# One weight block of 512 columns for the first 256 features of the feed-forward layers

## The chip, the core and the metric

The kernel runs on one core of a Trainium2 chip. The metric is the device time of one launch in microseconds (us), lower is better. The engines named below are TensorE (PE, matmuls), ScalarE (ACT), VectorE (DVE), GpSimd (POOL) and SyncE (SP, which issues the loads of the weights). An engine works through its own instructions in a fixed order, and waits at an instruction until the semaphores that it names have come.

## What is computed

Two layers on 256 tokens of 1024 features, all in float32. Each layer is a feed-forward half-step, a token mixer and a second feed-forward half-step; the mixer is gated linear attention in the first layer and a gated delta rule in the second.

```python
def swiglu(h, w_in, w_out):                       # w_in 1024 x 5632, w_out 2816 x 1024
    g, u = jnp.split(h @ w_in, 2, axis=-1)
    return (jax.nn.silu(g) * u) @ w_out

for i in range(2):
    x = x + 0.5 * swiglu(rmsnorm(x, norm_w[i, 0]), ffn_w_in[i, 0], ffn_w_out[i, 0])
    h = rmsnorm(x, norm_w[i, 1])
    x = x + (gla_mixer if i == 0 else gdn_mixer)(h, ...)
    x = x + 0.5 * swiglu(rmsnorm(x, norm_w[i, 2]), ffn_w_in[i, 1], ffn_w_out[i, 1])
return rmsnorm(x, final_norm_w)
```

The change touches the product `h @ w_in` for the first 256 of the 2816 features: 256 gate columns of g and 256 value columns of u.

## The kernel before

Six stages follow each other: f00, gla, f01, f10, gdn, f11 (a feed-forward layer is f and its layer and half). Every float32 product is made of three matmuls in a faster format: a weight is split into a rounded high part `hi` and the rest `lo`, the normalized and transposed activations `xT` likewise, and the products are xT high by hi, xT high by lo and xT low by hi.

The class `Weights` (`W`) feeds all stages with one stream of weight parts, numbered through the program (the four of the first columns of f01 are parts 99 to 102, for instance). SP loads raw blocks of 1 MB or 512 KB into 4 rotating buffers (`RAWS`). A part is 128 x 1024 values of a block: ACT rounds it to `hi` (line 69), DVE subtracts to get `lo` (line 76). 7 parts are kept (`LOOK`). The program text asks for the casts at chosen places: `high(n, held)` makes up to n casts on ACT, but none beyond `taken - held + LOOK`, where `taken` is the number of parts that `W.take` has handed out so far; `low` makes the next one on DVE. If `take` finds its part not yet cast, it makes it on the spot. So how many parts have been taken when `high` is called decides how far the casts run ahead, and with that in which place among an engine's other work each later cast stands.

Within a stage the 256 tokens are two halves, t = 0 and t = 1. A stage opens with its first columns, both halves over the same four weight parts; the opening is written out by hand in `step_over` (end of the stage before, transposes, `fill` of the first units of t = 0, then `low()` and `high(2, 4)`) and `second_half` (the rest of t = 0, `st.first(0)`, the units of t = 1 with `mids` between them, `st.first(1)`). `first` takes the accumulated columns out of PSUM: in a feed-forward layer with a Silu on ACT and a multiplication on DVE (lines 461 and 463), in gla with a scaled copy on ACT (line 623), in gdn with a Silu on ACT. The first stage has its own opening near the end of `trunk`.

In gla and gdn the first columns are `first_columns`: four parts of 2 row blocks (k) by 512 columns, matmuls of 512 columns, one PSUM buffer of two banks (`gup`) per half of the tokens of which one bank is used. In a feed-forward layer they are `FeedForward.part`: four parts of 4 row blocks by 256 columns (gate and value parts by turns, c = 0 and 1), matmuls of 256 columns (lines 445 to 447), one `gup` buffer per half with gate columns in one bank and value columns in the other. After the first columns, a feed-forward layer goes on with `ps_f` (lines 341 and 342: a matmul of 512 and one of 256 columns by turns, one part for each buffer); its matmul order is made by a scheduler of the framework from the program's dependencies. gla goes on with its gates, `ps_gk` and `tm_v` columns; gdn with convolved columns `ps_d` (lines 576 to 578, hi, hi, lo), for which DVE does a convolution (line 947) and copies (line 936), and with a chain on POOL and DVE that inverts triangular matrices (`Lm`, lines 1012 to 1034).

Of the kernel before, what the change touches and what calls it, by code (L numbers as in the profile page):

```python
# [11 lines left out]
AF = mybir.ActivationFunctionType  # L12
# [3 lines left out]
P = 128  # L16
# [11 lines left out]
class Weights:  # L28
# [15 lines left out]
    def _load(self, upto):  # L44
        while self.loaded < min(upto + 1, len(self.raws)):
            src, shape = self.raws[self.loaded]
            t = self.raw_pool.tile([P, 2048], F32, tag="raw", name=f"raw{self.loaded}")
            n = shape[0] * shape[1]
            tv = t[:, :n].rearrange("p (a b) -> p a b", b=shape[1])
            self.nc.sync.dma_start(tv, src)  # L50
            self.raw_tiles[self.loaded] = tv
            self.loaded += 1
# [55 lines left out]
def trunk(ctx: ExitStack, tc: tile.TileContext, x_in, norm_w, ffn_w_in, ffn_w_out, gla_w_in, gla_w_gk, gla_b_gk,  # L108
# [59 lines left out]
    for st in stages:  # L168
        if st[0] == "f":
            w1, w2 = ffn_w_in[int(st[1]), int(st[2])], ffn_w_out[int(st[1]), int(st[2])]  # L170
            for i in range(2):
                for c in (0, FF):
                    sub_rows(blk(w1, i * 512, 512, c, 256), 0, 4, 256)
            wo = {}
# [207 lines left out]
    def first_columns(N, name, pss):  # L382

        parts = []

        def units(t):
            if t == 0:
                parts.extend(W.take() for _ in range(4))
            pss[t] = gup(f"tm_{name}{t}")[:, 0, :]
            for s in range(4):  # L390
                for k in range(2):
                    xh, xl = (N.xT[:, 2 * s + k, u + t * P:u + (t + 1) * P] for u in (0, 256))
                    hi, lo = parts[s]
                    nc.tensor.matmul(pss[t], lhsT=xh, rhs=hi[:, k, :], start=(s + k == 0), stop=False)
                    nc.tensor.matmul(pss[t], lhsT=xh, rhs=lo[:, k, :], start=False, stop=False)
                    nc.tensor.matmul(pss[t], lhsT=xl, rhs=hi[:, k, :], start=False, stop=(s == 3 and k == 1))
                    yield
                if t == 1:
                    low()
                    high(1, 3 - s)  # L400

        return units

# [24 lines left out]
    class FeedForward:  # L428
        factor, quarter, mids = 0.5, 4, {}

        def __init__(self, N):
            self.N, self.parts, self.ps, self.am, self.aTs = N, [], {}, [], {}

        def part(self, t, s, c):

            N, i = self.N, 2 * s + c
            while len(self.parts) <= i:
                self.parts.append(W.take())
            if t not in self.ps:
                self.ps[t] = gup(f"g0_{N.name}{t}")  # L440
            hi, lo = self.parts[i]
            for k in range(4):
                o = self.ps[t][:, c, 0:256]
                xh, xl = (N.xT[:, 4 * s + k, u + t * P:u + (t + 1) * P] for u in (0, 256))
                nc.tensor.matmul(o, lhsT=xh, rhs=hi[:, k, :], start=(s + k == 0), stop=False)  # L445
                nc.tensor.matmul(o, lhsT=xh, rhs=lo[:, k, :], start=False, stop=False)  # L446
                nc.tensor.matmul(o, lhsT=xl, rhs=hi[:, k, :], start=False, stop=(s == 1 and k == 3))  # L447
                yield

        def units(self, t):  # L450
            for s in range(2):
                for c in range(2):
                    yield from self.part(t, s, c)
                    if t == 1:
                        low()
                        high(1, 3 - 2 * s - c)

        def first(self, t):
            N, ps = self.N, self.ps[t]
            sl = small(f"sl0_{N.name}{t}", 256, tag="t1")  # L460
            nc.scalar.activation(sl, ps[:, 0, 0:256], AF.Silu, scale=N.r[t][:, 0:1])
            a = small(f"a0_{N.name}{t}", 256, tag="t1")
            nc.vector.scalar_tensor_tensor(a, ps[:, 1, 0:256], N.r[t][:, 0:1], sl, op0=ALU.mult, op1=ALU.mult)
            self.am.append(a)
            if t == 1:
                rows_bc(N)
# [128 lines left out]
    def gla(N):  # L595
# [29 lines left out]
        ps0 = {}  # L625
        st.units = first_columns(N, "v0", ps0)
        st.first = lambda t: v_evac(ps0[t], t, 0)
# [204 lines left out]
    def gdn(N):  # L832
# [62 lines left out]
        ps0, ev0 = {}, gate_evac(N, srn, 0, 4, nwb[:, 256:384])  # L895
        st.units = first_columns(N, "dr0", ps0)
        st.first = lambda t: hold.update({"finish": ev0(ps0[t], t, t == 1)})
# [563 lines left out]
    with manual():  # L1461
# [7 lines left out]
        if isinstance(st, FeedForward):  # L1469
            part = lambda *a: [None for _ in st.part(*a)]  # L1470
            part(0, 0, 0)
            for g in range(2):
                turn_x(N, 1, g)()
                high(1)
                low()
            part(0, 0, 1)
            parameters()
            rms(N, 0)
            for c in range(2):
                part(1, 0, c)  # L1480
            rms(N, 1)
            high(1)
            low()
            for t in range(2):
                for c in range(2):
                    part(t, 1, c)
                st.first(t)
                high(1)
                low()
# [50 lines left out]
```

## Time and profile before

| | |
|---|---|
| median of 3 runs | 1045.27 us (1044.95 to 1045.68) |
| the profiled execution | 1045.1 us, its span 1043.4 us, granted clock 0.998 |
| busy in the span | PE 1027.3, PE weight loads 892.0, DVE 701.0, ACT 590.4, POOL 212.6 us |
| weights and data moved | 180.26 MB, mean 173 GB/s |
| stages | f00 to about 195 us, gla to 308, f01 to 495, f10 to 682, gdn to 848, f11 to the end |

Times in the rows are us from the start of the span. A row of the timeline gives the start, the duration, the engine, the line and the operation, what is written and read, and, in brackets, how long the engine had been idle before and what ended that. Matmuls overlap: the time that one takes in a row of matmuls is the step from its start to the next one's start, which is shorter than its duration. "x2" means that the row stands for two instructions, one behind the other.

### The profile page before, as it was taken

Reading aid. Unit: us, or ns where it says so; the run is one execution under the profiler, and the core shown is the slowest. Engines: PE = TensorE matmul, PEld = TensorE weight load, DVE = VectorE, ACT = ScalarE, POOL = GpSimd, SP = SyncE. Lnnn points to the kernel's source line nnn. Section 1 sums busy time; section 2 is a strip of 40 time slices with the busy share of each in tenths; the row PEclk is TensorE's granted clock in tenths of the full one; section 3 lists DMA queues with packets and bytes.
Section 4 is the critical chain, followed back from the end, with each engine's and each line's share of the span. In section 5 each row is a group of like instructions: output and inputs, shape, how many; then the busy total and the mean of one; then the engine's idle time right before and its main releaser. Section 6 shows DMA issues by size and latency. Waiting matters only on the chain.

```text
span 1043.4 us, 15585 instructions
## 1 busy us (share of the span) xinstructions
PE 1027.3 (98%) x6162; PEld 892.0 (85%) x6162; DVE 701.0 (67%) x956; ACT 590.4 (57%) x1019; POOL 212.6 (20%) x250
## 2 busy tenths in 40 slices
PE   8999999999999999999999999999999999999996
PEld 8888888789889888888988888879989898888885
DVE  5866666666577666666766666578998776666664
ACT  7655555573556555555655555478677565555552
POOL 2111111103201111110111111117734401111111
PEclk9999999999999999999999999999999999999999
DMA  8764645444364564744564655544443156556431
GB/s 295 242 235 139 231 158 172 155 130 158 141 222 162 202 212 152 240 139 148 210 233 155 209 175 188 164 125 135 144 135 131 47 198 240 191 173 216 147 122 41
DMA packets 132410, 180.26 MB, mean 173 GB/s; under 512 B 5212, under 2 KB 111760, under 8 KB 132336
## 3 DMA queue, kind: packets, MB, share of 16 engines
q1 hardware_dynamic: 131712, 178.14, 51.0%
q0 software_dynamic: 416, 0.84, 0.4%
q8 instruction: 48, 0.79, 0.3%
q10 hardware_dynamic: 208, 0.29, 0.1%
q14 instruction: 26, 0.21, 0.1%
HBM read 178.20 MB, written 1.05 MB: 172 GB/s over the span
## 4 chain that ended last, share of the span: by engine, by line
PE 91%; DVE 3%; POOL 2%; issue 1%; DMA 1%; ACT 1%; SPq 0%; POOLq 0%; DVEq 0%; ACTq 0%
PE ps_f L341 29%; PE ps_f L342 15%; PE acc_f L414 7%; PE acc_f L413 7%; PE acc_f L415 7%; PE ps_d L576 2%; PE g_f L445 1%; PE g_f L447 1%; PE g_f L446 1%; PE ps_d L578 1%; PE ps_d L577 1%; DMA x<-in_x_dram 1%; POOL Mc L1002 1%; DVE lo L76 1%; PE acc_gdn L415 1%
## 5 line engine op out<-in xcount | busy, mean ns | idle before, releaser
L76 DVE TENSOR_TENSOR lo<-raw,hi 128x1024 fp32r<-128x1024 f32 x336 | 431.4, 1297 | 198.8 <-ACT hi L69 198.7
L69 ACT CAST hi<-raw 128x1024 fp32r<-128x1024 f32 x338 | 348.1, 1046 | 190.6 <-PE acc_f L415 83.7
L341 PE MATMUL ps_f<-xT_f,hi 128*128 128x512 f32 x1280 | 455.6, 398 | 0.0
L342 PE MATMUL ps_f<-xT_f,lo 128*128 128x256 f32 x1280 | 359.1, 281 | 0.0
L341 PEld LDWEIGHTS ps_f<-xT_f,hi 128*128 128x128 f32 x1280 | 240.5, 188 | 58.4
L342 PEld LDWEIGHTS ps_f<-xT_f,lo 128*128 128x128 f32 x1280 | 241.7, 189 | 2.8
L371 POOL TENSOR_TENSOR pair_f<-plo_f,Rb_f 128x512 f32<-128x512 f32 x76 | 102.8, 1352 | 558.6 <-DVE plo_f L369 558.6
L413 PE MATMUL acc_f<-hi,aT_f 128*128 128x512 f32 x352 | 138.4, 393 | 0.0
L414 PE MATMUL acc_f<-lo,aT_f 128*128 128x512 f32 x352 | 137.9, 392 | 0.0
L415 PE MATMUL acc_f<-hi,aT_f 128*128 128x512 f32 x352 | 137.0, 389 | 0.0
L413 PEld LDWEIGHTS acc_f<-hi,aT_f 128*128 128x128 f32 x352 | 66.1, 188 | 15.1
L415 PEld LDWEIGHTS acc_f<-hi,aT_f 128*128 128x128 f32 x352 | 66.1, 188 | 14.4
L414 PEld LDWEIGHTS acc_f<-lo,aT_f 128*128 128x128 f32 x352 | 66.1, 188 | 10.7
L405 ACT CAST aT_f<-a_f 128x256 fp32r<-128x256 f32 x80 | 32.5, 407 | 71.6 <-DVE a_f L483 71.4
L481 ACT ACTIVATE sl_f<-pair_f 128x256 f32<-128x256 f32 x80 | 33.5, 418 | 54.6 <-POOL pair_f L371 48.6
L369 DVE TENSOR_TENSOR plo_f<-ps_f,plo_f 128x512 f32<-128x512 f32 x80 | 54.7, 683 | 12.6 <-ACT plo_f L368 12.5
L406 DVE TENSOR_TENSOR aT_f<-a_f,aT_f 128x256 fp32r<-128x256 f32 x80 | 34.0, 425 | 36.0 <-ACT aT_f L405 36.0
L576 PE MATMUL ps_d<-xT_gdn,hi 128*128 128x256 f32 x192 | 56.5, 294 | 0.1
L578 PE MATMUL ps_d<-xT_gdn,lo 128*128 128x256 f32 x192 | 54.4, 283 | 1.1 <-DVE lo L76 1.1
L577 PE MATMUL ps_d<-xT_gdn,hi 128*128 128x256 f32 x192 | 54.2, 282 | 0.0
L368 ACT COPY plo_f<-ps_f 128x512 f32<-128x512 f32 x80 | 46.4, 580 | 12.8 <-PE ps_f L342 12.8
L483 DVE TENSOR_TENSOR a_f<-sl_f,pair_f 128x256 f32<-128x256 f32 x80 | 33.0, 413 | 10.4 <-ACT sl_f L481 10.4
(363 smaller groups left out, 1299.0 us busy)
## 6 DMA issues: line engine op xcount, KB each, us to landing
raw<-in_ffn_w_in_dram SPq DMA_DIRECT2D x80, 1024.0 KB, 5.4
raw<-in_ffn_w_out_dram SPq DMA_DIRECT2D x44, 1024.0 KB, 5.4
raw<-in_gdn_w_in_dram SPq DMA_DIRECT2D x16, 1024.0 KB, 5.4
raw<-in_gla_w_in_dram SPq DMA_DIRECT2D x12, 1024.0 KB, 5.1
raw<-in_ffn_w_in_dram SPq DMA_DIRECT2D x16, 512.0 KB, 3.5
raw<-in_gla_w_out_dram SPq DMA_DIRECT2D x4, 1024.0 KB, 5.0
raw<-in_gdn_w_out_dram SPq DMA_DIRECT2D x4, 1024.0 KB, 5.0
out_dram<-fin SPq DMA_DIRECT2D x3, 256.0 KB, 2.1
```

The lines of the kernel that those rows point to most:

```text
L69: nc.scalar.copy(hv, src)
L76: self.nc.vector.tensor_tensor(lv, src, hv.bitcast(F32), op=ALU.subtract)
L341: nc.tensor.matmul(ps, lhsT=hi[:, k, :], rhs=N.xT[:, k, :], start=(k == 0), stop=False)
L342: nc.tensor.matmul(ps[:, 0:256], lhsT=lo[:, k, :], rhs=N.xT[:, k, 0:256], start=False, stop=(k == KT - 1))
L369: nc.vector.tensor_tensor(t, ps[:, :, 0:256], t, op=ALU.add)
L371: (eng or nc.gpsimd).tensor_tensor(dst, t, N.Rb.unsqueeze(1).broadcast_to([P, 2, 256]), op=ALU.mult)
L413: nc.tensor.matmul(accs[t][n], lhsT=ah, rhs=hi[:, 0, c], start=first, stop=False)
L414: nc.tensor.matmul(accs[t][n], lhsT=ah, rhs=lo[:, 0, c], start=False, stop=False)
L415: nc.tensor.matmul(accs[t][n], lhsT=al, rhs=hi[:, 0, c], start=False, stop=last)
L576: nc.tensor.matmul(o, lhsT=hi[:, k, :], rhs=xh, start=(k == 0), stop=False)
L577: nc.tensor.matmul(o, lhsT=hi[:, k, :], rhs=xl, start=False, stop=False)
L578: nc.tensor.matmul(o, lhsT=lo[:, k, :], rhs=xh, start=False, stop=(k == KT - 1))
```

## The change

The raw blocks of the first 256 features hold 2 row blocks by 256 gate and 256 value columns (two load instructions each) instead of 4 row blocks by 256 columns of one kind. A feed-forward layer now uses `first_columns`, with matmuls of 512 columns. `first_columns` asks for one `gup` buffer for both halves of the tokens, t = 0 in its first bank and t = 1 in its second, and takes a weight part from `W` when its first matmul is written instead of all four at the start; both hold for gla and gdn too. The lines of the new file stand 5 lower at its top and 11 higher further on (the cast `lo` is line 81, the first columns lines 401 to 403, `ps_f` lines 346 and 347).

```diff
@@ Weights._load
-            self.nc.sync.dma_start(tv, src)
+            if len(src.shape) == 3:
+                self.nc.sync.dma_start(tv, src)
+            else:
+
+                for a in range(shape[0]):
+                    self.nc.sync.dma_start(tv[:, a, :].rearrange("p (c f) -> p c f", c=src.shape[2]), src[:, a])
@@ the weight stream
-            for i in range(2):
-                for c in (0, FF):
-                    sub_rows(blk(w1, i * 512, 512, c, 256), 0, 4, 256)
+            for i in range(4):
+                w4 = w1[i * 256:(i + 1) * 256, :].rearrange("(k p) (c f) -> p k c f", p=P, c=2)
+                sub_rows(W.add_raw(w4[:, :, :, 0:256], (2, 512)), 0, 2, 512)
@@ first_columns
+        def part(t, s):
+            while len(parts) <= s:
+                parts.append(W.take())
+            if not pss:
+                both = gup(f"tm_{name}")
+                pss.update({0: both[:, 0, :], 1: both[:, 1, :]})
+            for k in range(2):
+                xh, xl = (N.xT[:, 2 * s + k, u + t * P:u + (t + 1) * P] for u in (0, 256))
+                hi, lo = parts[s]
+                nc.tensor.matmul(pss[t], lhsT=xh, rhs=hi[:, k, :], start=(s + k == 0), stop=False)
+                nc.tensor.matmul(pss[t], lhsT=xh, rhs=lo[:, k, :], start=False, stop=False)
+                nc.tensor.matmul(pss[t], lhsT=xl, rhs=hi[:, k, :], start=False, stop=(s == 3 and k == 1))
+                yield
+
         def units(t):
-            if t == 0:
-                parts.extend(W.take() for _ in range(4))
-            pss[t] = gup(f"tm_{name}{t}")[:, 0, :]
             for s in range(4):
-                for k in range(2):
...
-                    yield
+                yield from part(t, s)
                 if t == 1:
                     low()
                     high(1, 3 - s)
 
-        return units
+        return part, units
@@ FeedForward
-        factor, quarter, mids = 0.5, 4, {}
+        factor, quarter, mids = 0.5, 2, {}
...
+            self.part, self.units = first_columns(N, f"g0_{N.name}", self.pss)
@@ FeedForward.first
-            nc.scalar.activation(sl, ps[:, 0, 0:256], AF.Silu, scale=N.r[t][:, 0:1])
+            nc.scalar.activation(sl, ps[:, 0:256], AF.Silu, scale=N.r[t][:, 0:1])
-            nc.vector.scalar_tensor_tensor(a, ps[:, 1, 0:256], N.r[t][:, 0:1], sl, op0=ALU.mult, op1=ALU.mult)
+            nc.vector.scalar_tensor_tensor(a, ps[:, 256:512], N.r[t][:, 0:1], sl, op0=ALU.mult, op1=ALU.mult)
```

PE in f01, where the first columns pass from t = 0 to t = 1 (`g0_f010` and `g0_f011` are their buffers; `hi99` to `hi102` are the four parts, 103 is the next one). Before:

```order
1609 L447 MATMUL g0_f010_2861<-hi102_2793,xT_f01_2796 128x256
1610 L445 MATMUL g0_f010_2861<-hi102_2793,xT_f01_2796 128x256
1611 L446 MATMUL g0_f010_2861<-lo102_2794,xT_f01_2796 128x256
1612 L447 MATMUL g0_f010_2861<-hi102_2793,xT_f01_2796 128x256
1613 L445 MATMUL g0_f011_2955<-hi99_2733,xT_f01_2796 128x256 [waits Activation_49]
1614 L446 MATMUL g0_f011_2955<-lo99_2734,xT_f01_2796 128x256
1615 L447 MATMUL g0_f011_2955<-hi99_2733,xT_f01_2796 128x256 [waits DVE_49]
```

The same place on PE after the change (one buffer `tm_g0_f01` for both halves):

```order
1539 L402 MATMUL tm_g0_f01_2819<-lo102_2752,xT_f01_2754 128x512
1540 L403 MATMUL tm_g0_f01_2819<-hi102_2751,xT_f01_2754 128x512
1541 L346 MATMUL ps_f01_2_2942<-xT_f01_2754,hi103_2869 128x512 [waits DVE_49,PE_49,Activation_49]
1542 L347 MATMUL ps_f01_2_2942<-xT_f01_2754,lo103_2870 128x256 [waits DVE_49]
1543 L346 MATMUL ps_f01_2_2942<-xT_f01_2754,hi103_2869 128x512
1544 L347 MATMUL ps_f01_2_2942<-xT_f01_2754,lo103_2870 128x256
1545 L401 MATMUL tm_g0_f01_2819<-hi99_2691,xT_f01_2754 128x512 [waits DVE_49]
1546 L402 MATMUL tm_g0_f01_2819<-lo99_2692,xT_f01_2754 128x512
1547 L403 MATMUL tm_g0_f01_2819<-hi99_2691,xT_f01_2754 128x512
```

Four matmuls of `ps_f`, which need part 103, moved ahead of t = 1, and t = 1 now waits for DVE; before, no matmul of `ps_f` stood ahead of it. f10 and f11 read the same; in f00 it is eight matmuls of `ps_f`, ahead of the last 12 of t = 1.

DVE in gla, around its gate work (`gla_mem`, lines 718 to 728 before). Before:

```order
163 L718 TENSOR_SCALAR gla_mem4_1848<-psg_2073,vcol_109 128x256 x4
164 L76 TENSOR_TENSOR lo75_2054<-raw40_1970,hi75_2053 128x1024
165 L725 TENSOR_TENSOR gla_mem4_1848<-gla_mem4_1848,gla_mem0_1844 128x1024
166 L726 SCALAR_TENSOR_TENSOR gla_mem1_1845<-gla_mem1_1845,gla_mem4_1848 128x1024
167 L728 TENSOR_TENSOR gla_mem0_1844<-gla_mem1_1845 128x1024
168 L76 TENSOR_TENSOR lo76_2096<-raw40_1970,hi76_2095 128x1024
169 L76 TENSOR_TENSOR lo77_2124<-raw41_1974,hi77_2123 128x1024
```

After:

```order
162 L707 TENSOR_SCALAR gla_mem4_1803<-psg_2021,vcol_111 128x256 x4
163 L81 TENSOR_TENSOR lo74_2002<-raw39_1790,hi74_2001 128x1024
164 L714 TENSOR_TENSOR gla_mem4_1803<-gla_mem4_1803,gla_mem0_1799 128x1024
165 L715 SCALAR_TENSOR_TENSOR gla_mem1_1800<-gla_mem1_1800,gla_mem4_1803 128x1024
166 L717 TENSOR_TENSOR gla_mem0_1799<-gla_mem1_1800 128x1024
167 L81 TENSOR_TENSOR lo75_2046<-raw40_1925,hi75_2045 128x1024
168 L81 TENSOR_TENSOR lo76_2072<-raw40_1925,hi76_2071 128x1024
169 L81 TENSOR_TENSOR lo77_2093<-raw41_1967,hi77_2092 128x1024
```

The cast of part 75 moved from ahead of the three gate operations to behind them, and each cast stands where the next part's stood.

DVE in gdn, in the middle of the convolved columns (`Mc`, `Lm`: the start of the chain that inverts). Before:

```order
557 L76 TENSOR_TENSOR lo248_6825<-raw131_6542,hi248_6824 128x1024
558 L76 TENSOR_TENSOR lo249_6924<-raw131_6542,hi249_6923 128x1024
559 L947 SCALAR_TENSOR_TENSOR cv_d4_6966<-xp_d4_6965,vcol_109,cv_d4_6966 128x255 x2
560 L947 SCALAR_TENSOR_TENSOR cv_d4_6966<-xp_d4_6965,vcol_109,cv_d4_6966 128x254 x2
561 L947 SCALAR_TENSOR_TENSOR cv_d4_6966<-xp_d4_6965,vcol_109,cv_d4_6966 128x253 x2
562 L985 SCALAR_TENSOR_TENSOR E_6199<-G3_6989,krr3_6995,E_6199 128x128 x4
563 L1002 COPY Mc_6205<-E_6199 32x2x16x4 x4
564 L1012 STREAM_TRANSPOSE Lm_7045<-Mc_6205 128x512
565 L1013 TENSOR_SCALAR Lm_7045<-Lm_7045,side_104 128x256
566 L1014 SCALAR_TENSOR_TENSOR Lm_7045<-Lm_7045,side_104 128x256
567 L936 TENSOR_TENSOR xp_d5_7121<-ps_d5_6952,Rb_gdn_6355 128x512
568 L76 TENSOR_TENSOR lo250_6929<-raw132_6618,hi250_6928 128x1024
```

After:

```order
556 L81 TENSOR_TENSOR lo247_6682<-raw130_6396,hi247_6681 128x1024
557 L81 TENSOR_TENSOR lo248_6783<-raw131_6472,hi248_6782 128x1024
558 L936 SCALAR_TENSOR_TENSOR cv_d4_6823<-xp_d4_6822,vcol_111,cv_d4_6823 128x255 x2
559 L936 SCALAR_TENSOR_TENSOR cv_d4_6823<-xp_d4_6822,vcol_111,cv_d4_6823 128x254 x2
560 L936 SCALAR_TENSOR_TENSOR cv_d4_6823<-xp_d4_6822,vcol_111,cv_d4_6823 128x253 x2
561 L974 SCALAR_TENSOR_TENSOR E_6063<-G3_6846,krr3_6852,E_6063 128x128 x4
562 L991 COPY Mc_6069<-E_6063 32x2x16x4 x4
563 L1001 STREAM_TRANSPOSE Lm_6902<-Mc_6069 128x512
564 L1002 TENSOR_SCALAR Lm_6902<-Lm_6902,side_106 128x256
565 L1003 SCALAR_TENSOR_TENSOR Lm_6902<-Lm_6902,side_106 128x256
566 L925 TENSOR_TENSOR xp_d5_6978<-ps_d5_6809,Rb_gdn_6212 128x512
567 L81 TENSOR_TENSOR lo249_6786<-raw131_6472,hi249_6785 128x1024
```

The cast of part 249 moved behind the convolution of `cv_d4`, the work on E, Mc and Lm and the copy `xp_d5`. The order of the matmuls on PE is the same as before in gla and in gdn, but for one matmul.

## Rows read from the trace of the kernel before

**Rows 1.** The page, parts 1 and 4: busy time of each engine, and the chain.
```profile
PE 1027.3 (98%) x6162; PEld 892.0 (85%) x6162; DVE 701.0 (67%) x956; ACT 590.4 (57%) x1019; POOL 212.6 (20%) x250
...
PE 91%; DVE 3%; POOL 2%; issue 1%; DMA 1%; ACT 1%; SPq 0%; POOLq 0%; DVEq 0%; ACTq 0%
```

**Rows 2.** The waits of PE: engine, line, waited for, us in total, times, longest.
```profile
PE ps_d L578 <- DVE lo L76: 1.1, 2, 0.6
PE g_f L445 <- ACT hi L69: 1.0, 1, 1.0
...
PE Y L1048 <- ACT U L1036: 0.8, 1, 0.8
PE rb_gla L334 <- POOL rstd_gla L297: 0.7, 1, 0.7
...
PE U L1060 <- DVE YT L1053: 0.4, 1, 0.4
```

**Rows 3.** Timeline of PE, first columns of gla, matmuls of 512 columns.
```profile
203.15 0.39 PE L395 MATMUL tm_v<-lo,xT_gla 128*128 128x512 f32 x1
...
204.74 0.39 PE L396 MATMUL tm_v<-hi,xT_gla 128*128 128x512 f32 x1
```

**Rows 4.** Timeline of PE, DVE and ACT in f01, t = 1's first columns.
```profile
315.07 0.28 PE L445 MATMUL g_f<-hi,xT_f 128*128 128x256 f32 x1
...
320.83 0.38 PE L334 MATMUL rb_f<-ident,rstd_f 128*128 128x128 f32 x2
...
314.73 1.21 DVE L76 TENSOR_TENSOR lo<-raw,hi 128x1024 fp32r<-128x1024 f32 x1
315.86 0.47 DVE L463 SCALAR_TENSOR_TENSOR a_f<-g_f,rstd_f,sl_f 128x256 f32<-128x256 f32 x1
...
315.33 0.48 ACT L461 ACTIVATE sl_f<-g_f,rstd_f 128x256 f32<-128x256 f32 x1 [0.86 <-PE g_f L447]
```

**Rows 5.** Timeline of PE, ACT and DVE at the same handover in f00.
```profile
23.15 0.38 PE L334 MATMUL rb_f<-ident,rstd_f 128*128 128x128 f32 x2
...
21.81 0.47 ACT L461 ACTIVATE sl_f<-g_f,rstd_f 128x256 f32<-128x256 f32 x1
...
20.40 1.23 DVE L76 TENSOR_TENSOR lo<-raw,hi 128x1024 fp32r<-128x1024 f32 x1 [0.73 <-ACT hi L69]
22.32 0.48 DVE L463 SCALAR_TENSOR_TENSOR a_f<-g_f,rstd_f,sl_f 128x256 f32<-128x256 f32 x1 [0.69 <-ACT sl_f L461]
```

**Rows 6.** Timeline of POOL, ACT and DVE, first columns of gla.
```profile
200.27 0.55 POOL L297 TENSOR_TENSOR rstd_gla<-ms_gla,mhalf 128x1 f32<-128x1 f32 x1 [15.43 <-DVE ms_gla L295]
204.23 1.66 POOL L297 TENSOR_TENSOR rstd_gla<-ms_gla,mhalf 128x1 f32<-128x1 f32 x1 [3.41 <-DVE ms_gla L295]
...
204.54 0.69 ACT L623 ACTIVATE v<-tm_v,rstd_gla 128x512 f32<-128x512 f32 x1 [0.54 <-PE tm_v L396]
...
204.26 1.22 DVE L76 TENSOR_TENSOR lo<-raw,hi 128x1024 fp32r<-128x1024 f32 x1
```

**Rows 7.** Timeline of PE and DVE in gla, part 75 and the gate work.
```profile
226.00 0.28 PE L578 MATMUL ps_gk<-xT_gla,lo 128*128 128x256 f32 x1
...
220.75 1.21 DVE L76 TENSOR_TENSOR lo<-raw,hi 128x1024 fp32r<-128x1024 f32 x1
...
227.46 2.35 DVE L76 TENSOR_TENSOR lo<-raw,hi 128x1024 fp32r<-128x1024 f32 x2
```

**Rows 8.** Timeline of PE and DVE in gdn, parts 249 and 250.
```profile
746.49 0.28 PE L578 MATMUL ps_d<-xT_gdn,lo 128*128 128x256 f32 x1
...
749.23 2.41 DVE L76 TENSOR_TENSOR lo<-raw,hi 128x1024 fp32r<-128x1024 f32 x2
```

**Rows 9.** Timeline of PE and DVE in gdn, parts 255 and 256.
```profile
765.86 0.28 PE L578 MATMUL ps_d<-xT_gdn,lo 128*128 128x256 f32 x1
...
765.95 0.69 DVE L1024 TENSOR_TENSOR Lm<-Lm,side 128x512 f32<-128x512 f32 x1 [0.76 <-POOL Lm L273]
...
771.75 2.35 DVE L76 TENSOR_TENSOR lo<-raw,hi 128x1024 fp32r<-128x1024 f32 x2
```

**Rows 10.** Timeline of SP at the start: issuing loads of raw blocks.
```profile
1.71 0.98 SPq L50 DMA_DIRECT2D raw<-in_ffn_w_in_dram  x2
```

More of the change, by code (lines that the diff above doesn't have):

```diff
@@ L384, in first_columns @@
         parts = []
+        def part(t, s):
[11 more added lines that the diff above has]
+                yield
         def units(t):
-            if t == 0:
-                parts.extend(W.take() for _ in range(4))
-            pss[t] = gup(f"tm_{name}{t}")[:, 0, :]
             for s in range(4):
-                for k in range(2):
[L392 to L396, printed above, removed]
-                    yield
+                yield from part(t, s)
                 if t == 1:
@@ L428, in trunk @@
     class FeedForward:
-        factor, quarter, mids = 0.5, 4, {}
+        factor, quarter, mids = 0.5, 2, {}
         def __init__(self, N):
[L432 to L456, printed above, removed]
+            self.N, self.pss, self.am, self.aTs = N, {}, [], {}
+            self.part, self.units = first_columns(N, f"g0_{N.name}", self.pss)
         def first(self, t):
-            N, ps = self.N, self.ps[t]
+            N, ps = self.N, self.pss[t]
             sl = small(f"sl0_{N.name}{t}", 256, tag="t1")
-            nc.scalar.activation(sl, ps[:, 0, 0:256], AF.Silu, scale=N.r[t][:, 0:1])
+            nc.scalar.activation(sl, ps[:, 0:256], AF.Silu, scale=N.r[t][:, 0:1])
             a = small(f"a0_{N.name}{t}", 256, tag="t1")
-            nc.vector.scalar_tensor_tensor(a, ps[:, 1, 0:256], N.r[t][:, 0:1], sl, op0=ALU.mult, op1=ALU.mult)
+            nc.vector.scalar_tensor_tensor(a, ps[:, 256:512], N.r[t][:, 0:1], sl, op0=ALU.mult, op1=ALU.mult)
             self.am.append(a)
@@ L625, in gla @@
         ps0 = {}
-        st.units = first_columns(N, "v0", ps0)
+        _, st.units = first_columns(N, "v0", ps0)
         st.first = lambda t: v_evac(ps0[t], t, 0)
@@ L895, in gdn @@
         ps0, ev0 = {}, gate_evac(N, srn, 0, 4, nwb[:, 256:384])
-        st.units = first_columns(N, "dr0", ps0)
+        _, st.units = first_columns(N, "dr0", ps0)
         st.first = lambda t: hold.update({"finish": ev0(ps0[t], t, t == 1)})
@@ L1470, in trunk @@
             part = lambda *a: [None for _ in st.part(*a)]
-            part(0, 0, 0)
+            part(0, 0)
             for g in range(2):
@@ L1475, in trunk @@
                 low()
-            part(0, 0, 1)
+            part(0, 1)
             parameters()
             rms(N, 0)
-            for c in range(2):
-                part(1, 0, c)
+            for s in range(2):
+                part(1, s)
             rms(N, 1)
@@ L1484, in trunk @@
             for t in range(2):
-                for c in range(2):
-                    part(t, 1, c)
+                for s in (2, 3):
+                    part(t, s)
                 st.first(t)
```

## The prediction

> **What bounds the kernel now.** I read the busy times first, then the chain of work that ended last, then what PE waited for, then the timeline around the places that the change touches. PE is busy for 1027.3 of 1043.4 us and holds 91% of the chain [rows 1]: there is almost no idle time on PE, and its list of waits is short, with no wait over 1.1 us in total outside the start [rows 2]. So two things change the time: matmul time that is saved comes off the end in full, and any new wait of PE is added in full unless a wait behind it shrinks. In this kernel the sum of an edit is therefore: matmul steps saved, plus new waits of PE, less old waits that they swallow.
>
> **The wider matmuls.** In f01, t = 1's 48 matmuls of 256 columns run from 315.07 to 320.83 [rows 4], 0.120 us each. A matmul of 512 columns takes (204.74 − 203.15) / 7 = 0.227 us, from the eight that stand between the two rows, ends included [rows 3]. Two narrow ones, 0.240, become one wide, 0.2275: 0.0125 us saved, 48 times a layer, 0.6 us in each of four layers, 2.4 us in all. The Trainium skill, page "TensorE: Matmul & The Clock Gate", section "Back-to-back issue gap", gives 2.5 ns per matmul beside the columns' own time; the pair would then save only 2.5 ns, an estimate of 0.5 us for all four layers, and the sum would be 1.9 us higher. The trace decides against it: by these steps a matmul of either width costs some 13 ns beside its columns at the 2.4 GHz level (granted clock 0.998), and dropping one drops those 13.
>
> **The loads.** The same bytes come in 32 load instructions instead of 16. Inside the program a block is asked for four buffers ahead, tens of us before its cast, so I cost this at nothing. At the start nothing hides it: two issues on SP take 0.98 us [rows 10], so PE's first matmul, which already waits 1.0 us for its weight [rows 2], could come up to 0.5 us later, and the x block behind four issues instead of two up to 1 us. The bytes ahead of both are the same and are what is waited for, so I take 0; the range keeps +0.5. The Trainium skill, page "DMA: Bandwidth & Descriptors", section "Measured (HBM→SBUF, 128 partitions, SWDGE, issued from GpSimd)", advises batches of 1 MiB or more, which speaks against cutting 512 KB in two; no row here prices it, and by it the end that I keep would be the likelier one.
>
> **The common buffer.** t = 0 and t = 1 are now one buffer, so t = 1's first matmul is made to wait for the evacuation of t = 0, although they use different banks. Before, PE ran from t = 0 into t = 1 without a stop. In f01, t = 0 ends 24 × 0.0125 = 0.3 us earlier, at about 314.8. PE goes to the four `ps_f` matmuls that were moved forward. The second of these needs `lo` of part 103, which DVE makes from 314.73 to 315.94 [rows 4]: PE waits 0.9 us there, has done the four at about 316.4, by which time the multiplication at 315.86 + 0.47 = 316.33 has freed t = 0's bank. t = 1 takes 24 × 0.228 = 5.5 us, to 321.9. Before, `rb_f` stood at 320.83; the four `ps_f` matmuls (0.12 + 0.23 by turns, 0.7 us) are now behind us. Net 321.9 − 0.7 − 320.83 = +0.35 us. f10 and f11 have the same pattern: **+1.05 us** for the three. What is queued behind the wait is the whole of PE; DVE and ACT aren't held.
>
> In f00 the handover is later on ACT: its Silu runs at 21.81 and the multiplication ends at 22.32 + 0.48 = 22.80 [rows 5]. t = 0 ended at 23.15 − 24 × 0.12 = 20.27, now at about 19.8; the second of eight `ps_f` matmuls waits for the `lo` that ends at 20.40 + 1.23 = 21.63, the eight are done at about 22.9, and the last 12 of t = 1 end at 25.6. Before, 23.15 plus the eight (1.4 us) was 24.55: **+1.0 us**.
>
> In gla, t = 0 is evacuated by ACT from 204.54 to 205.23 [rows 6]. t = 1's first three matmuls, 0.68 us, then end at 205.95, and one short matmul later PE stands at the row that today waits 0.7 us for `rstd` on POOL [rows 2], at 205.9. That `rstd` takes 1.66 us beside a `lo` cast of DVE and 0.55 us alone [rows 6]; the cast is moved away from there, so the new wait takes the old one's place: **+0.15 us**. gdn repeats it with **+0.1**.
>
> **The casts that slide.** This is the largest part, and it isn't in the feed-forward layers at all. When `step_over` calls `high(2, 4)`, gla and gdn have now taken two parts fewer, so one cast fewer is made there. From then on each cast, on ACT and on DVE, stands in the next part's place, in gla from part 71 on and in gdn from part 236 on, until later code catches up. PE's order hasn't moved. A cast that had more than one place of slack doesn't matter; I went through all parts, comparing PE's first use of `lo` with the end of the next part's `lo`. Those that come out negative by more than 0.1 us, and aren't covered by the delay that another one makes, are three.
>
> Part 75 in gla: PE needs `lo` at 226.00. It was made at 220.75; its new place is that of part 76, the first of two casts at 227.46, so about 228.67, behind the gate work [rows 7]. **+2.7 us**, with nothing behind it to swallow it. ACT's high part is made earlier and doesn't hold.
>
> Part 249 in gdn: needed at 746.49, its new place is the first of two at 749.23, done about 750.45 [rows 8]: a wait of 4.0 us. Before, PE waited 0.7 us for part 250 just behind [rows 2], which goes: **+3.3 us**.
>
> Part 255: needed at 765.86, new place 771.75, done about 772.95 [rows 9], behind the end of POOL's chain at 765.95. 7.1 us, of which PE's delay of 3.3 already covers a part: 3.8. Behind it PE waited today for ACT's U (0.8), for `lo` (0.45 of the 1.1) and for DVE's YT (0.4) [rows 2], which go, since DVE and ACT aren't later there: **+2.2 us**. Part 247 and its neighbours add 0.1.
>
> **Sum.** −2.4 is already inside the feed-forward nets; so 1.05 + 1.0 + 0.15 + 0.1 + 2.7 + 3.3 + 2.2 + 0.1 = +10.6 us. Made against the profiled execution, 1045.1 + 10.6 = **1055.7 us**; the median of the runs is 0.17 us higher, which I leave out. Bounds: part 255's wait is 2.2 if DVE keeps its times and up to 7.1 if its work is pushed back as PE is; part 75's is 1.5 if DVE's gate work starts as soon as a cast leaves its way, 2.7 otherwise; the handovers lie between −2.4 (no wait binds) and +2.5.
>
> **Rivals.** (a) The handover waits bind, but the casts that slide don't: ACT and DVE are idle for a third of the time [rows 1] and run ahead of where they stood. Then 1045.1 + 2.3 = 1047.4. Against it: on DVE the operations ahead of parts 75, 249 and 255 run without a pause of over 0.8 us (the 0.76 in [rows 9] is one of the longest), so there is nothing to run ahead into. (b) Only the gain: neither the late casts nor the handovers bind, since PE finds its weights and its buffer ready when it comes. 1045.1 − 2.4 = 1042.7, which is faster than before. For it: ACT's 0.69 us in gla is short. Against it: in a feed-forward layer 0.48 + 0.47 us stand behind the last matmul of t = 0, plus a cast, and PE has four matmuls for it. It decides if the evacuation takes under 0.7 us. (c) Only one mixer pays: gla 2.7 or gdn 5.6 beside the handovers, 1050.1 or 1053.0. For it: gdn's POOL chain sets the place of part 255, and its operations last 0.3 or 1.1 us, depending on what DVE does beside them. (d) DVE's places in gdn slide back with PE, since its copies `xp_d` need PE's columns: part 255 costs its 7.1 in full, 1060.6.
>
> **How the numbers follow.** The forecast, all three casts late and own range 1053.5 to 1059, has 0.55. (c) 0.17, (d) 0.12, (a) 0.10, (b) 0.06. The range 1048 to 1060.5 holds the forecast, (c) and a good part of (d), and leaves out (a), (b) and the rest of (d), about 0.2. A measurement of this kernel can tell 0.2%, 2.1 us, from no change: same is 1043.2 to 1047.4, which (a) touches from above and half of it falls in; with a little from (b), same has 0.07, faster 0.05, slower 0.88.
>
> **What would show it.** In the profile after, PE's waits should name DVE's `lo` for `ps_gk` (one wait of 2.7) and for `ps_d` (two of about 4), three of about 0.9 and one of 1.7 for `lo` at the moved `ps_f` matmuls, and `rb_gla` should wait no longer. The matmuls of the first columns should step by 0.227 us. I am wrong about the sliding casts if PE has no wait at these three parts, about the handovers if t = 1 follows without a gap, and about the size if DVE's gate work or POOL's chain stands at other times than before, measured from the stage's start.

## The result, and the profile after

| | before | after |
|---|---|---|
| median | 1045.47 us (1044.95 to 1046.16, 4 runs) | 1062.07 us (1058.46 to 1065.28, 4 runs) |
| ratio | | 1.0157, 95% interval 1.0123 to 1.0192 |
| profiled execution, its span | 1045.1, 1043.4 us | 1065.28, 1063.0 us |
| granted clock, mean | 0.998 | 0.986 |

The change costs 16.6 us, 1.6%. The forecast was 1055.7 with a range to 1060.5: the sign is right, and the measured time lies 1.6 us above the range. The four executions of the changed kernel spread over 6.8 us, those of the kernel before over 1.2, and the mean granted clock goes with the time: 0.986, 0.990, 0.992 and 0.995 for 1065.3, 1063.0, 1061.1 and 1058.5 us. That is the first trace of what the forecast lacks. The profiled execution, from which the rows below come, is the slowest of the four.

The page of the changed kernel, against [rows 1]: busy times, the granted clock in 40 slices, and the chain.

```profile
PE 1035.1 (97%) x5970; PEld 889.3 (84%) x5970; DVE 703.4 (66%) x956; ACT 590.6 (56%) x1019; POOL 208.7 (20%) x250
...
PEclk8999999999999999999999999999889999999998
...
PE 89%; DVE 3%; ACT 2%; POOL 2%; issue 1%; DMA 1%; SPq 0%; POOLq 0%; ACTq 0%; DVEq 0%
```

192 fewer matmul instructions keep PE busy for 7.8 us longer. Before, every slice of the clock row was a 9:

```profile
PEclk9999999999999999999999999999999999999999
```

Now the first, two in gdn and the last are an 8. PE's last matmul falls into the last slice, and the clock is low behind it.

What PE waits for now (engine, line, waited for, us in total, times, longest), against [rows 2]:

```profile
PE ps_d L567 <- DVE lo L81: 7.1, 2, 3.6
PE ps_gk L567 <- DVE lo L81: 2.6, 1, 2.6
PE xps_f L317 <- DMA x<-in_x_dram: 2.1, 1, 2.1
PE ps_f L347 <- DVE lo L81: 2.0, 3, 0.7
...
PE tm_g_f L401 <- DVE a_f L452: 1.0, 1, 1.0
PE tm_v L401 <- ACT v L612: 0.8, 1, 0.8
PE tm_dr L401 <- ACT gdn_srn L537: 0.8, 1, 0.8
```

This is nearly the list that the prediction wrote down: one wait for `ps_gk`, two for `ps_d`, three at the moved `ps_f` matmuls, `rb_gla` gone. The fourth at `ps_f`, 1.7 us for `lo` in f00, is missing; there PE waits 1.0 us for the multiplication (`a_f`). New is the third row: PE waits 2.1 us for the second x block, where it waited 0.3 before.

Timeline of PE and DVE at the three late parts, against [rows 7 to 9] (idle time before an instruction in brackets):

```profile
233.25 0.39 PE L567 MATMUL ps_gk<-xT_gla,lo 128*128 128x256 f32 x1 [2.56 <-DVE lo L81]
...
231.98 2.35 DVE L81 TENSOR_TENSOR lo<-raw,hi 128x1024 fp32r<-128x1024 f32 x2
...
760.18 0.58 PE L567 MATMUL ps_d<-xT_gdn,lo 128*128 128x256 f32 x1 [3.60 <-DVE lo L81]
760.56 0.41 PE L565 MATMUL ps_d<-xT_gdn,hi 128*128 128x256 f32 x1
760.77 0.41 PE L566 MATMUL ps_d<-xT_gdn,hi 128*128 128x256 f32 x1
...
758.90 2.40 DVE L81 TENSOR_TENSOR lo<-raw,hi 128x1024 fp32r<-128x1024 f32 x2
...
784.76 0.58 PE L567 MATMUL ps_d<-xT_gdn,lo 128*128 128x256 f32 x1 [3.46 <-DVE lo L81]
...
783.49 2.35 DVE L81 TENSOR_TENSOR lo<-raw,hi 128x1024 fp32r<-128x1024 f32 x2
```

Each wait ends with the first of DVE's two casts in a row, as forecast (for part 75: 231.98 and half of 2.35 is 233.2). But the matmuls of 256 columns behind 760.18 step by 0.21 us instead of 0.12. The stretches around these places, with the granted clock as the third number from the end:

```profile
12.00:19.00 7.00, 6.10 (x19) 5.10 (x20) 4.82 (x11) 4.94 (x15) 0.00 (x0) 0.51 1.12 384
...
234.00:238.00 4.00, 4.00 (x23) 4.00 (x23) 2.43 (x3) 4.00 (x5) 0.00 (x0) 0.59 0.60 181
...
760.00:766.00 6.00, 5.82 (x27) 5.82 (x28) 4.48 (x10) 3.52 (x7) 4.98 (x14) 0.50 0.57 178
...
784.00:790.00 6.00, 5.24 (x24) 5.24 (x25) 2.63 (x4) 2.65 (x7) 0.00 (x0) 0.50 0.56 177
```

0.50 is the lower of TensorE's two levels, 1.2 instead of 2.4 GHz. The clock falls in each of the four waits of over 2 us (2.11, 2.56, 3.60 and 3.46) or shortly behind it, and nowhere else while PE works; before, it fell only after PE's last matmul. Where the 19.6 us of the profiled execution come from can be read by comparing the starts of the same instructions in both traces:

| from start to ... | forecast | after: lag gained |
|---|---|---|
| f00, to its transposes `a0t` | +1.0 | +4.4 |
| gla, first columns, to `ps_z` | +0.15 | +0.1 |
| gla, part 75, to `ps_gq` | +2.7 | +4.3 |
| f01 | +0.35 | +0.3 |
| f10 | +0.35 | +0.25 |
| gdn, first columns | +0.1 | +0.2 |
| gdn, part 249 | +3.4 with part 247 | +5.7 |
| gdn, part 255, to the first U matmul | +2.2 | +4.0 |
| f11 and the end | +0.35 | +0.4 |

Five terms hold within 0.1 us. The other four are too small by 1.6 to 3.4 us, and they are the four with a wait of over 2 us.

### The profile page after: what moved, and what is told of

Same layout as the page of the kernel before. It is cut to its first block, busy times and chain, and to the rows that moved or that the text cites. A ratio compares the mean times of both kernels' runs of the same rounds, so it can differ in the third digit from the quotient of the medians.

```text
span 1063.0 us, 15259 instructions
## 1 busy us (share of the span) xinstructions
PE 1035.1 (97%) x5970; PEld 889.3 (84%) x5970; DVE 703.4 (66%) x956; ACT 590.6 (56%) x1019; POOL 208.7 (20%) x250
## 4 chain that ended last, share of the span: by engine, by line
PE 89%; DVE 3%; ACT 2%; POOL 2%; issue 1%; DMA 1%; SPq 0%; POOLq 0%; ACTq 0%; DVEq 0%
PE ps_f L346 28%; PE ps_f L347 14%; PE acc_f L425 7%; PE acc_f L424 7%; PE acc_f L426 7%; PE ps_d L565 2%; PE ps_d L567 1%; PE ps_d L566 1%; PE tm_g_f L401 1%; PE tm_g_f L403 1%; PE tm_g_f L402 1%; DVE lo L81 1%; POOL Mc L991 1%; DMA x<-in_x_dram 1%; PE acc_gla L426 1%
## 5 line engine op out<-in xcount | busy, mean ns | idle before, releaser
L376 POOL TENSOR_TENSOR pair_f<-plo_f,Rb_f 128x512 f32<-128x512 f32 x76 | 99.9, 1314 | 565.8 <-DVE plo_f L374 565.8
L567 PE MATMUL ps_d<-xT_gdn,lo 128*128 128x256 f32 x192 | 57.0, 297 | 7.1 <-DVE lo L81 7.1
L565 PE MATMUL ps_d<-xT_gdn,hi 128*128 128x256 f32 x192 | 58.6, 305 | 0.0
L566 PE MATMUL ps_d<-xT_gdn,hi 128*128 128x256 f32 x192 | 56.3, 293 | 0.0
L567 PEld LDWEIGHTS ps_d<-xT_gdn,lo 128*128 128x128 f32 x192 | 39.1, 203 | 7.6 <-DVE lo L81 7.5
```

Source lines behind the costliest of these rows:

```text
L376: (eng or nc.gpsimd).tensor_tensor(dst, t, N.Rb.unsqueeze(1).broadcast_to([P, 2, 256]), op=ALU.mult)
L565: nc.tensor.matmul(o, lhsT=hi[:, k, :], rhs=xh, start=(k == 0), stop=False)
L566: nc.tensor.matmul(o, lhsT=hi[:, k, :], rhs=xl, start=False, stop=False)
L567: nc.tensor.matmul(o, lhsT=lo[:, k, :], rhs=xh, start=False, stop=(k == KT - 1))
```

## The experiments

The theory after this reading: the waits are as forecast; behind a wait of over 2 us PE also runs some us at the half clock, in some executions and not in others; and in f00 the x block comes late because of the loads. The rivals: the terms themselves were too small; the clock has another cause; f00's loss is the handover between the halves of the tokens.

### One part alone: taking late

```diff
-            if t == 0:
-                parts.extend(W.take() for _ in range(4))
...
             for s in range(4):
+                while len(parts) <= s:
+                    parts.append(W.take())
```

(in the kernel before; only gla and gdn use this function there)

> The kernel before, with one part of the change alone: gla and gdn take a weight part when its first matmul is written. DVE and ACT have the casts in gla and gdn as in the changed kernel; the feed-forward layers are as before. Theory (a wait of PE of over 2 us costs its length and then some us at the half clock): part 75 costs 4.3, parts 249 and 255 cost 5.4 and 4.0 as the trace of the changed kernel shows, less nothing else: +13.5 us, 1058 to 1060, with the granted clock at its low level behind each of the three waits, and runs that spread by some us. Rival 1 (the slid casts cost their waits alone, and the rest comes from the wide matmuls or the loads): 2.7 + 3.3 + 2.2 = +8.2, 1053.5, granted clock 0.998 as before. Rival 2 (late taking is harmless): 1045 to 1047.

Measured: 1054.14 us (1051.44 to 1055.5), ratio 1.0077 (1.006 to 1.0093). PE's waits:

```profile
PE ps_d L578 <- DVE lo L76: 7.2, 2, 3.6
PE ps_gk L578 <- DVE lo L76: 2.6, 1, 2.6
```

The same three waits to 0.1 us as in the changed kernel, so the slid casts make them, without a common buffer, wide matmuls or new loads. The total is below the theory's 1058 to 1060 and near rival 1's 1053.5, for two reasons that the trace shows. The half clock came in part only (stretches of this kernel; the third number from the end is the clock):

```profile
229.00:233.00 4.00, 4.00 (x36) 4.00 (x35) 2.36 (x2) 4.00 (x5) 0.00 (x0) 1.00 0.70 225
...
751.00:756.00 5.00, 4.33 (x23) 4.33 (x24) 4.24 (x8) 4.00 (x9) 4.29 (x10) 0.66 0.60 177
```

Behind part 75's wait of 2.56 us the clock stayed at its upper level this time, and part 75 cost 2.8 us instead of 4.3. In gdn it fell behind both waits, and the two places cost 4.5 (249 with 247) and 3.1 us, more than the 3.4 and 2.2 of the waits alone; so it is the trace that speaks against rival 1, not the total. And `rb_gla` and `rb_gdn` no longer wait for `rstd`: taking late gains 0.9 us in each of the two stages, a gain that the common buffer eats up in the changed kernel.

### The changed kernel with early taking

```diff
-            while len(parts) <= s:
+            while len(parts) <= max(s, ahead):
                 parts.append(W.take())
...
-        _, st.units = first_columns(N, "v0", ps0)
+        _, st.units = first_columns(N, "v0", ps0, 3)
```

(`ahead` is 0 in the feed-forward layers; gdn likewise)

> The changed kernel, but gla and gdn take their four parts at the start again, so that the casts stand where they stood before; the blocks, the wide matmuls and the common buffer stay. Theory: the three waits and the low clock behind them go, 13.7 us; what is left is f00's 4.4, 0.1 in gla, 0.3, 0.4 and 0.5 in the other feed-forward layers and 0.2 in gdn: about 1051. Rival 1 (only the waits go, the low clock has another cause): 1062 - 8.2 = 1054 or more, with low clock still in gla or gdn. Rival 2 (the common buffer makes waits of its own once the casts are early): over 1053.

Measured: 1050.76 us (1049.39 to 1051.47), ratio 1.0046 (1.0031 to 1.0061). The three waits and the low clock in gla and gdn are gone, 11.3 us at the median. What is left is f00: by its trace +4.5 of +5.3 us stand before the transposes of f00.

### Early taking and own buffers

```diff
-            if not pss:
-                both = gup(f"tm_{name}")
-                pss.update({0: both[:, 0, :], 1: both[:, 1, :]})
+            if t not in pss:
+                pss[t] = gup(f"tm_{name}{t}")[:, 0, :]
```

> As the run before (early taking), and each half of the tokens has its own PSUM buffer, so that no evacuation is waited for. Left of the change are the blocks (with their 32 loads) and the wide matmuls. Theory: the handovers' 0.3 to 0.5 us per layer turn into the 0.6 us gain of the wide matmuls, and f00 keeps the later x block with some low clock: f01, f10, f11 -1.8, f00 +1 to +3, so 1044.5 to 1046.5. Rival (f00's 4.4 us are the handover, not the x block): f00 gains 0.6 too, 1042.7. Rival 2 (the buffer is no cause, nothing changes against the run before): 1051.

Measured: 1046.05 us (1044.6 to 1046.96), ratio 1.0005 (0.9995 to 1.0014). f01, f10 and f11 each come out 0.7 us faster than before, so the wide matmuls gain at least the 0.6 that was worked out for them. But f00 still loses 3.75 us, more than the theory's 1 to 3, with no handover to wait for; PE's wait for x is even longer:

```profile
13.92 1.97 PE L317 MATMUL xps_f<-ident,x 128*128 128x128 f32 x8 [3.28 <-DMA x<-in_x_dram]
```

So f00's loss is mostly the late x block and the half clock behind it: these eight transposes take 1.97 us, before 1.10.

### The loads: cut in two, and cut in which way

The kernel before, with each of the four blocks loaded by two instructions:

```diff
-            self.nc.sync.dma_start(tv, src)
+            if shape == (4, 256):
+                for a in (0, 2):
+                    self.nc.sync.dma_start(tv[:, a:a + 2, :], src[:, a:a + 2, :])
+            else:
+                self.nc.sync.dma_start(tv, src)
```

> The kernel before, with one part alone: the four raw blocks of the first columns of each feed-forward layer are loaded with two instructions of 256 KB instead of one of 512 KB; nothing else. Theory: at the start the second x block is issued some 1.6 us later behind four issues, lands about 0.9 us later, PE waits about 1 to 2 us for it and falls to the half clock: +1 to +3 us, all of it before 25 us. Rival 1 (the loads are hidden, f00's loss is the handover): within 0.3 us of before. Rival 2 (smaller loads cost in every feed-forward layer): waits on loads in f01, f10 and f11 too.

Measured: 1045.22 us, ratio 0.9999 (0.999 to 1.0009). The theory's number was wrong and the rival's right: twice as many loads cost nothing, x is there at 11.8 us. That leaves the form of the changed kernel's loads, each of which takes one row block of gate and of value columns. The same blocks cut by kind instead, beside early taking and own buffers:

```diff
-                for a in range(shape[0]):
-                    self.nc.sync.dma_start(tv[:, a, :].rearrange("p (c f) -> p c f", c=src.shape[2]), src[:, a])
+                for c in range(src.shape[2]):
+                    self.nc.sync.dma_start(tv[:, :, c * 256:(c + 1) * 256], src[:, :, c])
```

> As the run with early taking and own buffers, but the two loads of a raw block are cut by column kind (two row blocks by 256 gate columns, then by 256 value columns) instead of by row block; the same bytes land at the same places. Theory (the form of the load, not the number of loads, brings the second x block late in f00): x lands before 12 us as with the split loads of the kernel before, no wait of PE over 2 us, clock at its high level, and all four layers gain 0.6: 1042.7. Rival (the x block is late because of four issues ahead of it or by chance): x lands at about 13 or later, 1046 as in that run.

Measured: 1044.35 us (1042.33 to 1049.76, 12 runs), ratio 0.9992 (0.9981 to 1.0002). Timeline of SP, first with the changed kernel's loads (the run with own buffers), then with the loads by kind:

```profile
1.72 2.60 SPq L55 DMA_DIRECT2D raw<-in_ffn_w_in_dram  x4
4.36 0.60 SPq L222 DMA_DIRECT2D x<-in_x_dram  x1
```

```profile
1.71 1.96 SPq L55 DMA_DIRECT2D raw<-in_ffn_w_in_dram  x4
3.71 0.47 SPq L222 DMA_DIRECT2D x<-in_x_dram  x1
```

The stretch from 7 to 8 us of both (the last two numbers are the DMA engines' busy share and GB/s):

```profile
7.00:8.00 1.00, 0.76 (x8) 0.57 (x6) 0.80 (x4) 1.00 (x2) 0.14 (x2) 1.00 0.37 97
```

```profile
7.00:8.00 1.00, 1.00 (x7) 1.00 (x6) 0.97 (x4) 1.00 (x3) 0.14 (x2) 1.00 1.07 390
```

With row blocks an issue takes 0.65 us instead of 0.49, and in this stretch the DMA engines are partly empty; with loads by kind they are full, and x is there at 12.06 us instead of 13.92. The stretch is an extreme one (the changed kernel moved 275 GB/s in it), but the difference holds over more: from 4 to 10 us the five traces with loads by row block moved 223 to 243 GB/s, the five with loads by kind 274 to 293, the kernel before 275. The later issue of x makes up 0.65 us of the 1.86; the rest lies in the transfers. When x comes differs between executions: from 12.90 to 14.05 us with row blocks, from 11.5 or earlier to 12.76 by kind with x behind both blocks, 12.04 before. Why SP and the transfers need longer for that form isn't shown by these runs and stays open. The profiled execution takes 1043.04 us, 2.1 under that of before, close to the 2.4 that were expected; the median and the spread are not: PE still waits 1.6 us for x, since it is through with its first part earlier.

Issuing x behind the first raw block instead of the second:

```diff
-    W._load(1)
+    W._load(0)
     nc.sync.dma_start(x[:, 1, :], xv[:, 1, :])
+    W._load(1)
```

> As the run before it, and the load of the second x block is issued behind the first raw block instead of behind the second. Theory (x's landing is set by the bytes and issues ahead of it): x lands about 1 us earlier and PE waits less for it, but the second weight block lands later and PE waits for its high part instead: 1042 to 1043, within 0.7 us of the run before. Rival (the wait for x is the start's bound alone): 1 us faster than the run before.

Measured: 1044.69 us (1042.71 to 1046.01), 0.3 us from the run before it but above the expected 1042 to 1043. x is there at 10.4, but PE then waits 1.75 us for the high part of the second weight block: in one order PE waits for x, in the other for the weight, and neither is faster.

### The common buffer alone

The changed kernel with early taking and loads by kind:

> The changed kernel with early taking and with the loads cut by column kind; the common buffer stays. What the common buffer costs, with neither slid casts nor a late start: the forecast's terms, +1.0 in f00, +0.35 in each of the other three layers, +0.15 in gla and +0.1 in gdn: 1047.4. Rival (f00's loss was the handover all along): f00 still loses 4.4, 1050.7.

Measured: 1047.62 us (1046.73 to 1049.09), ratio 1.0022 (1.0012 to 1.0031); expected 1047.4. By its trace: f00 +1.3, f01 +0.3, f10 +0.3, gla and gdn +0.2 each, f11 +0.3. So the handover terms were right, f00's to 0.3 us.

### Filling the waits

The clock is the rest. If it falls because PE stands still, giving PE idle work there must keep it up.

```diff
             hi, lo = W.take()
+            for _ in range({75: 18, 249: 28, 255: 28}.get(W.taken - 1, 0)):
+                nc.tensor.matmul(ps[:, s, 0:P], lhsT=ident, rhs=ones, start=True, stop=True)
```

> The changed kernel with idle matmuls (ones by the identity, 128 columns, 0.12 us each) written on PE ahead of the first matmul of three weight parts: 18 ahead of part 75, 28 each ahead of parts 249 and 255. They fall into the three waits, so that PE works through most of them; their output is overwritten by the part's own first matmul. Theory (the granted clock falls to its low level because PE stood still there, and the low clock is what the sum lacked in gla and gdn): the clock stays at 2.4 GHz in gla and gdn, the three places cost 2.7, 3.3 and 2.2 us as forecast, and f00 keeps its 4.4: 1045.1 + 4.4 + 0.1 + 2.7 + 1.2 + 0.2 + 5.5 = 1059, with a smaller spread than the changed kernel's 7 us. Rival (the clock falls for another reason, such as the order of the matmuls behind): low clock behind the same places, 1062 or more, since the idle matmuls come on top.

Measured: 1063.74 us (1063.4 to 1063.95), ratio 1.0173 (1.016 to 1.0186). Each of these matmuls is two instructions in the trace, so the idle work was twice as long as meant (4.2 us for 18) and longer than the waits, which is why the time isn't lower: the total is the rival's. But the clock is the theory's, at 1.00 in all stretches behind the three places, and the spread has shrunk from 6.8 to 0.55 us. With the counts set right (10, 15, 15):

> The run with filled waits again, with idle matmuls that fit: each of them is two instructions in the trace, so that run's 18 and 28 took 4.2 and 6.4 us, longer than the waits; here 10, 15 and 15, about 2.3 and 3.5 us. Theory: the clock stays high in gla and gdn, the three places cost the forecast 2.7, 3.3 and 2.2 us, f00 about 4: 1058 to 1059.5, with a spread of about 1 us. Rival: the waits cost what they cost in the changed kernel, 1062, whatever PE does meanwhile.

Measured: 1058.36 us (1056.88 to 1059.54), ratio 1.0117 (1.0094 to 1.0141). PE works more than in the changed kernel and the kernel is 3.7 us faster at the median. The spread is 2.7 us, not about 1. The wait for x in f00 is still open here, 2.66 us, and the clock still falls behind it; but so it is in the run before, with 2.38 us, whose spread is 0.55, so what makes this spread isn't settled. Part 75 costs 2.85 us, 249 with 247 3.0 and 255 2.2, against 4.3, 5.7 and 4.0: the half clock was worth 6.0 us in the profiled execution of the changed kernel, and about 3.7 at the median.

The last step takes away the late x block too: the changed kernel with loads by kind, those idle matmuls, and six more behind the first part of f00, where PE waits for x. Common buffer and late taking stay.

> The changed kernel, common buffer and late taking as they are, with the loads cut by column kind and idle matmuls in the wait for x (6) and in the three long waits (10, 15, 15): nothing is left of the late x block and of the low clock. Theory (the forecast's terms were right and what it lacked is the clock and the start): 1055.7, the forecast, within 1 us, clock at its high level in all stages. Rival (the terms themselves were too small): 1058 or more.

Measured: 1055.33 us (1055.25 to 1055.83), ratio 1.009 (1.0068 to 1.0112). The forecast's terms alone, with neither the late x nor the half clock, give the forecast's time to 0.4 us, and the spread is 0.6 us. By its trace f00 costs 0.65 us (forecast 1.0), the first columns of gla 0.1 (0.15), part 75 2.85 (2.7), f01 and f10 together 0.6 (0.7), the first columns of gdn 0.2 (0.1), part 249 with 247 3.0 (3.4), part 255 2.4 (2.2), f11 and the end 0.4 (0.35). Its clock behind the three places:

```profile
229.00:234.00 5.00, 4.67 (x39) 4.49 (x38) 3.42 (x4) 5.00 (x8) 0.00 (x0) 1.00 0.45 132
752.00:757.00 5.00, 4.73 (x41) 4.53 (x40) 4.93 (x9) 3.09 (x8) 3.25 (x6) 1.00 0.11 24
775.00:780.00 5.00, 4.01 (x35) 3.81 (x34) 4.58 (x7) 3.49 (x7) 0.00 (x0) 1.00 0.21 34
```

### A version that beats both

Wide matmuls without what they brought along: early taking, own buffers, loads by kind, and the six idle matmuls before the second x block, written into the bank that t = 1's first matmul overwrites.

```diff
             part(0, 0)
+            if 1 not in st.pss:
+                st.pss[1] = gup("tm_first1")[:, 0, :]
+            for _ in range(6):
+                nc.tensor.matmul(st.pss[1][:, 0:P], lhsT=ident, rhs=ones, start=True, stop=True)
```

> Early taking, own buffers, loads by column kind, and 6 idle matmuls (1.4 us) on PE ahead of the transposes of the second x block, where PE waits 1.6 us at the start; their output is overwritten. Theory (the spread of 1042.3 to 1049.8 without them is the clock that falls in some executions behind that wait): the range closes to about 1 us, median 1042.5 to 1043.2, faster than before by 0.2%. Rival (the spread has another cause): median about 1044.4 and a spread of several us again.

Measured: 1042.94 us (1042.06 to 1043.61, 12 runs), ratio 0.9972 (0.9961 to 0.9982). 2.5 us faster than before, near the 2.4 us that the wide matmuls were worth on paper; but the match is partly luck. The profiled execution is 1.8 us faster than that of before: f01, f10 and f11 gain 0.6 to 0.7 us each, and f00 gains nothing (its transposes start 0.1 us later), since x is there only at 12.76 us. Without the idle matmuls, the same kernel spread from 1042.3 to 1049.8; with them over 1.6 us. That they closed the range isn't shown: 11 of those 12 executions lie below 1046.2, and the kernel before, which has no such wait, has one in 17 at 1051.67 us with the same mean clock of 0.990 as the one at 1049.76. What is seen is a median 1.4 us lower. What PE waits for is again much like the list of [rows 2], with x at 1.1 us.

## Why the prediction was right and wrong

The order of the reading held: PE bounds the kernel, so every wait counts in full. Step by step:

- **The wide matmuls**, 2.4 us by the steps of [rows 3, 4]: right in three layers. f01, f10 and f11 gain 0.6 to 0.7 us each where no handover stands against it; in f00 the start hides or takes back the gain (0.4 with loads by kind, none in the best version). The rule that the prediction set against it, an estimate of 0.5 us by the Trainium skill, page "TensorE: Matmul & The Clock Gate", section "Back-to-back issue gap", is not what this kernel shows.
- **The common buffer**, +2.3 us: right, +2.2 with early taking and loads by kind (1047.62 against 1045.4 before). Single terms are off by at most 0.3 us; in f01 PE waited 0.67 us for `lo` instead of 0.9.
- **The casts that slide**, 2.7, 3.3 and 2.2 us with 0.1 for part 247: right where the clock is held, 2.85, 3.0 and 2.4. Rivals (a), (b) and (c), in which late casts don't bind, and (d), in which part 255 costs 7.1 us, are out: the two waits in gdn are 3.6 and 3.5 us.
- **The loads**, taken as nothing with an end of +0.5: this step failed. "The bytes ahead of both are the same and are what is waited for" is true of bytes, but the changed loads are of a form that SP issues in 0.65 us, 0.16 more than the same bytes by kind. Going from one form to the other is worth 3.1 us with early taking (1050.76 to 1047.62) and 3.0 with the waits filled (1058.36 to 1055.33, with six idle matmuls in the wait for x besides). In the profiled execution of the changed kernel most of this isn't the landing itself: against the common-buffer run, x is there 0.6 us later in the changed kernel (12.90 against 12.29), and from there to the transposes `a0t` PE needs 2.5 us more, with a clock of 0.50 behind its wait of 2.11 us. In other executions the shares differ: with the three waits filled, x is there at 14.05 and the clock costs about 1 us behind it. The bound was taken from [rows 10], where the loads were of another form; the row that would have bounded it wasn't in the trace of before, and the range should have been open there. The rule of the Trainium skill, page "DMA: Bandwidth & Descriptors", section "Measured (HBM→SBUF, 128 partitions, SWDGE, issued from GpSimd)", to batch loads to 1 MiB or more, pointed to the right place for another reason: the size of the loads costs nothing here, 1045.22 us with split loads against 1045.14 without.
- **The rule for the sum**, "matmul steps saved, plus new waits of PE, less old waits that they swallow": this is the other step that failed. It has no term for what follows a wait. Behind each of the three waits PE ran some 3 to 6.5 us at 1.2 GHz, which costs half of that where the work isn't waited out anyway: 3.7 us at the median (1062.07 against 1058.36 with the waits filled; the ranges of the two just overlap), and more where it follows the late x block. In the slowest execution, the profiled one, it is 6.0 us behind the three waits and about 2.5 in f00, 8.5 of the 9 us that the sum lacked. In [rows 2] no wait is long enough for this to be seen, and the clock of before is 0.998 throughout, which should have been a question: does it stay so when PE stands still for 4 us?

So of the 16.6 us, 9.9 are left when the half clock behind the three casts (3.7) and the late x block with the half clock behind it (3.0) are taken out one after the other; that they add up is in the nature of such a chain of runs, but that the 9.9 meet the forecast's 10.6, term by term to 0.4 us and in the same places, is not.

## What to carry to other kernels

A new wait of some us on TensorE can cost more than its length: here one of 2.56 us cost 2.8 us where the clock stayed up and 4.3 where it fell. Price it with the slow stretch behind it, and expect the time to spread. When a change makes a function take its inputs later, look at everything that counts how many have been taken: here a lazy `take` in a shared helper slid casts by one place in two stages that the change wasn't about, and cost over half of the loss. A change of layout should be costed with the form of its loads, not with their bytes.

## What the runs showed of the hardware

- The granted clock fell to 0.50 in, or shortly behind, waits of PE of 2.11, 2.38, 2.46, 2.66 and 3.28 us (for x), 2.56 us (in gla) and 3.46 to 3.62 us (in gdn), and in the profiled executions not behind those of up to 1.75 us (x and weight blocks at the start of the versions with loads by kind). Waits of about the same length could go either way: behind 2.56 us in gla it fell in the changed kernel and stayed in the run with late taking alone. The Trainium skill, page "TensorE: Matmul & The Clock Gate", section "What's actually happening", says that the low clock is the default and that activity lifts it; the runs agree in that idle matmuls in the waits hold it at 1.00, and the kernel is faster with the more work.
- The mean granted clock goes with the time of an execution (0.986 to 0.995 for 1065.3 to 1058.5 us in the changed kernel). The spread over four executions was 6.8 us with the waits open, 2.7 us with the three casts' waits filled and 0.55 with them overfilled (the one for x open in both), and 0.6 us with all four filled. The kernel before, without long waits, has one execution of 17 at 1051.67 us and 0.990; what lowered its clock isn't known.
- `rstd` on POOL, 1.66 us beside a cast of DVE in [rows 6], took 0.55 us at 208.52 in the changed kernel, where the cast of 128x1024 had moved away.
- Four loads of 256 KB, two for each 512 KB block, were issued in 2.60 or in 1.96 us, depending on whether one load takes both column kinds of a row block or one kind of two row blocks; from 4 to 10 us the DMA moved 223 to 243 GB/s with the first form and 274 to 293 with the second. The cause is open.
